# Seven-product retention projection and its gate columns: an order written out for three engines, and another way to add the attention branch in the last unit

## The chip, the core and the metric

The kernel runs on one core of one Trainium2 chip. A core has TensorE (PE, matrix products into PSUM banks), VectorE (DVE), ScalarE (ACT), GpSimd (POOL), SyncE (SP, which issues most loads) and 16 DMA engines. Each engine works through its own queue of instructions in order; engines wait for one another through semaphores. The metric is the time of one execution on the device in microseconds, lower is better. Times of several executions are given as their median with the lowest and the highest; where one execution was taken with the hardware profiler, its own time is named beside it.

## What is computed

One step of a one-layer hybrid backbone on 128 context tokens and 512 latent tokens, 640 in all, with 1024 channels, in fp32. Cut to the part that the change touches:

```python
def token_mixer(h, ...):
    q, k, v, rq, rk, rv, rg, ga, gr = split(h @ w_in)
    ya = attend_blocks(q, k_all, v_all)
    yr, s_f, s_b = retention_branch(rq, rk, rv, rg, ...)   # silu(rg) * rms_scale(o)
    y = sigmoid(ga) * (ya @ w_att_o) + sigmoid(gr) * (yr @ w_ret_o)
    return y @ w_out
```

Before it stand the conditioning, a normalisation, the attention and the retention scans; after it a gated residual, a second normalisation, a gated MLP with a width-3 convolution, another gated residual and a last normalisation. The sigmoids are computed as (1 + tanh(x/2)) with the factor one half folded into other constants. The stage of interest is `gr = h @ w_in[:, 5632:]`, `yr @ w_ret_o`, the gated sum of both branches, and the beginning of `y @ w_out`.

## The kernel before

**Numbers.** Every fp32 product is made of three reduced-precision matmuls: each operand is split into a high part (a cast) and a low part (the difference), and high x high, high x low and low x high are accumulated. So each weight block costs ScalarE a cast (L145, L1065) and VectorE a subtraction (L150, L1070) before TensorE can use it. For two of the seven products of a unit the low part is made in another way: ScalarE writes the negated value (L1067), and a DMA issued by GpSimd adds the weight to it while writing (L1068).

**Gate columns (L1031 to L1042).** The 1024 channels of `gr` are eight columns of 128. Each column is 48 matmuls of 320 tokens (two halves of 24), ScalarE takes the tanh of each half out of its bank (L1036). Weights come for two columns at a time: one load of a megabyte into a `raw` buffer (two of them, shared by all weight loads), then casts and subtractions into `wh` tiles (eight of them, shared by all weights). Between the quarters of the first columns TensorE transposes the retention output `yr` in ten blocks (`yr_blocks`), and behind column 1 `ret_sums` forms four sums of quarters of `yr` on VectorE (two or three passes each, then a cast on ScalarE and a subtraction on VectorE), with the last two rows of `thr` as scratch.

**Seven-product units (L1044 to L1157).** `yr @ w_ret_o` is a two-by-two block product done with seven products instead of eight. A unit `p` makes two columns (`f` 0 and 1) of 128 channels; there are four units, 28 products, each 12 matmuls of 320 tokens. `load` fetches a unit's weights, `prep(m)` makes the operand of one product (for four of the seven a sum of two weight quarters first, L1062), `prod(m)` runs it and takes its bank out: a copy or negated copy on ScalarE (L1096 to L1100, L1104, L1108) or an addition or subtraction on VectorE (L1102, L1105, L1111). Several products accumulate into the same bank without clearing it and are read in between, so the next product of that bank must wait until the bank has been read. `col(f)` multiplies a finished column with its gate (L1076) and then lets a GpSimd DMA add the attention branch, which was spilled to DRAM earlier as `thd`, onto it (L1077). `merge(f)` splits the finished column into the high and low operand `h2` of the next projection (L1082 on ScalarE, L1083 on VectorE).

**The order.** `seq` lists the 28 products. `ret_pump(n)` is called before the first product and after each; it emits loads and preparations as long as no more than eight prepared tiles are waiting for their product. `later` and `pend` hold a `col` for one product after the column is complete and a `merge` for eight products after. All of this is program text; what it fixes depends on the block around it. `tc.manual_schedule(engines={ET.PE})` (L1147) keeps the order of the text on TensorE alone. On the other engines, and for everything outside such a block, a planner lays the queue of each engine when the kernel is built, from its own estimate of when each instruction can start; that order is then fixed.

**Behind it.** The block ends with `gate_rows` (L1163): four groups of small matmuls into three banks, each copied out by ScalarE (L277). Then the output projection runs in two halves of 512 channels (`a_group`, L157 to L159, for the first; `out_half` for the second), its weights through the same `raw` and `wh` buffers, and the loads of the residual `x1` (L1184), of the convolution weights (L1273, L1274) and of the first block of `w_up` (L1253 casts it) queue up on SP.

Of the kernel before, what the change touches and what calls it, by code (L numbers as in the profile page):

```python
# [13 lines left out]
ALU = mybir.AluOpType  # L14
# [4 lines left out]
P = 128  # L19
# [50 lines left out]
def hybrid_step(ctx: ExitStack, tc: tile.TileContext, a: dict, o: dict):  # L70
# [937 lines left out]
    def ret_sums():  # L1008
        for m in (1, 2):
            t = f0(F32R)  # L1010
            ys[m] = [t[:, :, :HALF], t[:, :, HALF:]]
        ys[3] = [rt([P, 4, HALF], F32R) for _ in range(2)]
        x = thr[:, 6:8, :].rearrange("p a b -> p (a b)").rearrange("p (k t) -> p k t", k=4)
        q = {m: [z.bitcast(F32) for z in ya[m]] for m in ya}

        def diff(xs, zs):
            V.tensor_sub(x, xs[0], zs[0])
# [12 lines left out]

    for c in range(KD):  # L1031
        if c % 2 == 0:
            wg = load_w(w_in[:, O_GR + c * P:O_GR + (c + 2) * P], 8, 256)

        def gr_ev(hf, ts, ps, c=c):
            nc.scalar.activation(thr[:, c, ts], ps, AF.Tanh, scale=0.5)  # L1036
        for _ in b_col(wg, slice((c % 2) * P, (c % 2 + 1) * P), hTk, mm, gr_ev):
            for _ in range(2):
                next(yb, None)
        if c == 1:  # L1040
            run(yb)
            ret_sums()  # L1042

    def ret_unit(p):  # L1044
        st, ops, bs = {}, {}, {}
        u = [f1() for _ in range(2)]
        los, his = slice(0, HALF), slice(HALF, TOK)

        def load():
# [20 lines left out]
                V.tensor_sub(lo, src, hi.bitcast(F32))  # L1070
            ops[m] = (hi, lo)

        AOP = {1: ya[0, 0], 5: ys[1], 6: ys[2], 2: ya[0, 1], 7: ys[3], 4: ya[1, 1], 3: ys[4]}

        def col(f):
            V.scalar_tensor_tensor(u[f], thr[:, 2 * p + f, :], 1.0, u[f], op0=ALU.add, op1=ALU.mult)  # L1076
            nc.gpsimd.dma_start(u[f], thd[:, 2 * p + f, :], accum_op=ALU.add)  # L1077

        def merge(f):
            c = 2 * p + f  # L1080
# [4 lines left out]
        def prod(m):  # L1085
            q = {1: 1, 6: 1, 7: 1, 4: 1, 2: 2, 5: 3, 3: 3}[m]
            if m in (1, 2, 5):
                st[q] = mm([P, 512], tag="mm")[:, :HALF]
            ps, (ah, al), (bh, bl) = st[q], AOP[m], ops[m]
            for k in range(4):  # L1090
                nc.tensor.matmul(ps, bh[:, k], ah[:, k], start=m in (1, 2, 5) and k == 0, stop=False,
                                 skip_group_check=m in (3, 4, 6, 7))
                nc.tensor.matmul(ps, bh[:, k], al[:, k], start=False, stop=False, skip_group_check=m in (3, 4, 6, 7))
                nc.tensor.matmul(ps, bl[:, k], ah[:, k], start=False, stop=k == 3, skip_group_check=m in (3, 4, 6, 7))
            if m == 1:
                nc.scalar.copy(u[0][:, los], ps)  # L1096
            elif m == 5:
                nc.scalar.activation(u[1][:, his], ps, AF.Copy, scale=-1.0)
            elif m == 6:
                nc.scalar.activation(u[1][:, los], ps, AF.Copy, scale=-1.0)  # L1100
            elif m == 2:
                V.tensor_add(u[0][:, los], u[0][:, los], ps)  # L1102
            elif m == 7:
                nc.scalar.copy(u[0][:, his], ps)  # L1104
# [8 lines left out]
        return load, prep, prod  # L1113

    w_out = a["w_out"][0]
    later, pend, wo0 = [], [], []
# [13 lines left out]
    preps.append((KD // 2, 4, len(seq), lambda: wo0.append(w_split(wo0[0], 4, 512))))  # L1130
    done, loaded, live = 0, 0, []

    def ret_pump(n):
        nonlocal done, loaded
        while done < len(preps):
            g, tiles, last, fn = preps[done]
            if loaded <= min(g + 1, len(loads) - 1):
                loads[loaded]()
                loaded += 1
                continue  # L1140
            if sum(x for x, z in live if z >= n) + tiles > 8:
                return
            fn()
            live.append((tiles, last))
            done += 1

    with tc.manual_schedule(engines={ET.PE}):  # L1147
        ret_pump(0)
        for n, (p, m) in enumerate(seq):
            units[p][2](m)  # L1150
            pend.extend((n + d, fn) for d, fn in later)
            later.clear()
            ret_pump(n + 1)
            for x in [x for x in pend if x[0] <= n]:
                x[1]()
# [551 lines left out]
```

## Time and profile before

| what | value |
|---|---|
| median of 3 runs | 1203.02 us (1202.22 to 1203.61) |
| the profiled execution | 1202.9 us, of which the span from first to last instruction is 1201.1 us |
| TensorE busy | 1156.9 us, 96% of the span |
| VectorE, ScalarE, GpSimd busy | 774.7, 591.0 and 184.3 us |
| mean granted TensorE clock | 0.990 |
| gate columns | about 554.4 to 615.5 us of the span |
| seven-product units | about 615.5 to 678.9 us |
| gate rows, output projection (to the second row block of its second half) | about 678.9 to 730.8 us |

How to read the rows that follow. A row of busy time by stretch gives the stretch, its length, and the busy microseconds (with the number of instructions) of TensorE, its weight loads, VectorE, ScalarE and GpSimd, then the granted clock, the DMA engines' share and GB/s. A row of waits reads: engine, what it was about to write, line, `<-` whom it waited for, then the total, the number of times and the longest in us. A row of the timeline begins with start and duration in us; the bracket at its end is the idle time before it and what ended that. In the tables of transfers the last number is the median time from issue to landing in us. L numbers are lines of the kernel before.

### The profile page before, as it was taken

The page shows a single profiled execution, that of the slowest core. Times are in us where ns is not written, and L with a number is a line of the kernel's source. Part 1 is how long each engine was busy: PE and PEld are TensorE (multiplying, and loading weights), DVE is VectorE, ACT ScalarE, POOL GpSimd, SP SyncE. Part 2 cuts the span into 40 slices and gives each one's busy share as a digit, 9 for nine tenths or more (in the row PEclk, how much of TensorE's full clock was granted, in tenths as well). Part 3 has the DMA queues.
Part 4 walks back from the last instruction along what each step waited for, and adds up shares of the span by engine and source line. Part 5 has one row for each costly group of instructions (what it writes and reads, how often), then busy time and mean ns, then how long its engine had stood idle before and what let it go on. Part 6 is the DMA issues. An engine that isn't in the chain of part 4 may idle for free.

```text
span 1201.1 us, 18411 instructions
## 1 busy us (share of the span) xinstructions
PE 1156.9 (96%) x7269; PEld 1037.8 (86%) x7269; DVE 774.7 (64%) x1465; ACT 591.0 (49%) x1079; POOL 184.3 (15%) x193
## 2 busy tenths in 40 slices
PE   4999999999999999999998889999999999999996
PEld 4788899999988888888998767999989999899995
DVE  4566977765234436446755437977858677598887
ACT  4355655561132324444445324576657657475463
POOL 0042200000022000052022111011112112111113
PEclk9999999999999999999999998999999999999998
DMA  8742111126664431112247674536756558657553
GB/s 283 241 143 70 37 35 36 36 71 215 222 224 141 141 97 44 36 36 70 71 73 148 174 110 151 147 60 141 168 123 123 131 127 174 148 99 156 135 113 121
DMA packets 136936, 146.38 MB, mean 122 GB/s; under 512 B 26625, under 2 KB 102481, under 8 KB 136849
## 3 DMA queue, kind: packets, MB, share of 16 engines
q1 hardware_dynamic: 106592, 112.95, 29.0%
q0 software_dynamic: 30256, 32.25, 17.1%
q8 instruction: 57, 0.93, 0.3%
q14 instruction: 31, 0.25, 0.1%
HBM read 112.94 MB, written 8.65 MB: 101 GB/s over the span
## 4 chain that ended last, share of the span: by engine, by line
PE 41%; issue 5%; DVE 3%; DMA 2%; POOL 1%; ACT 1%; DVEq 0%; SPq 0%; POOLq 0%; ACTq 0%
DMA x1.u1.1_6470<-in_x_prompt 1%; DMA f1.s.14_5877<-spill.u2.2_2893 1%; POOL x1.u1.1_6470 L1194 1%; DVE acts.u2.2_97 L1222 0%; DMA f1.s.13_5876<-spill.u2.2_2893 0%; DVE acts.u1.1_96 L1221 0%; DVE x1.u1.1_6470 L1194 0%; ACT x1.u1.1_6470 L1386 0%; PE mm7.mm.45_9731 L1501 0%; PE mm7.mm.57_10483 L1501 0%; PE mm7.mm.9_7577 L1504 0%; PE mm7.mm.30_8750 L1501 0%; PE mm7.mm.42_9482 L1501 0%; PE mm7.mm.33_8999 L1501 0%; PE mm7.mm.63_10849 L1503 0%
## 5 line engine op out<-in xcount | busy, mean ns | idle before, releaser
L795 POOL DMA_DIRECT2D spill.u2.2_2893<-f1.s.1_1165 x1 | 0.6, 588 | 130.1 <-DVE mod.u4.4_2852 L586 130.1
L1515 DVE TENSOR_TENSOR t7.u4.4_7006<-t7.u4.4_7006,const.u1.1_70 128x322 f32<-128x322 f32 x10 | 4.9, 495 | 11.6 <-ACT const.u1.1_70 L1514 11.6
L888 DVE SCALAR_TENSOR_TENSOR ret2.u1.1_4329<-ret2.u1.1_4329,const.u13.13_93 64x128 f32<-64x128 f32 x24 | 6.8, 337 | 6.6 <-ACT ret2.u1.1_4329 L881 6.5
L1426 POOL TENSOR_TENSOR x1.u1.1_6470<-x1.u1.1_6470,weights.raw.422_11068 128x512 f32<-128x512 f32 x5 | 8.2, 1639 | 10.4 <-ACT x1.tm.112_11081 L1398 7.6
L890 DVE SCALAR_TENSOR_TENSOR ret2.u1.1_4329<-ret2.u1.1_4329,const.u13.13_93 64x128 f32<-64x128 f32 x24 | 6.6, 383 | 4.8 <-ACT ret2.u1.1_4329 L883 4.8
L841 DVE TENSOR_TENSOR ret.u5.5_3535<-ret.u5.5_3535,ret.u1.1_3528 128x512 f32<-128x512 f32 x5 | 3.5, 693 | 9.4 <-POOL ret.r2k.8_3713 L839 3.3
L841 DVE TENSOR_TENSOR ret.u4.4_3534<-ret.u4.4_3534,ret.u1.1_3528 128x512 f32<-128x512 f32 x5 | 3.5, 692 | 9.0 <-POOL ret.r2k.11_3893 L839 4.7
L412 ACT CAST acts.u1.1_96<-f0.s.1_109 128x640 fp32r<-128x640 f32 x4 | 2.9, 727 | 12.2 <-DVE f0.s.1_109 L410 12.2
L1068 POOL DMA_DIRECT2D weights.wh.156_5897<-weights.raw.151_5882 x1 | 1.4, 1352 | 47.3 <-ACT weights.wh.156_5897 L1067 47.3
L1254 DVE TENSOR_TENSOR gt.gt1.4_6666<-weights.raw.203_6663,gt.gt0.3_6665 128x1280 fp32r<-128x1280 f32 x1 | 1.5, 1494 | 10.9 <-ACT gt.gt0.3_6665 L1253 10.9
L565 POOL TENSOR_TENSOR p1.u1.1_609<-p1.u3.3_613,p1q.u1.1_603 128x512 f32<-128x512 f32 x1 | 1.3, 1303 | 46.4 <-DMA p1.vc.6_618<-in_cache_v 46.4
L374 PE MATMUL mm1.mm.1_167<-const.u1.1_70,xin.u1.1_108 128*128 128x128 f32 x4 | 1.1, 435 | 7.2 <-DVE xin.u1.1_108 L365 7.2
L412 ACT CAST acts.u1.1_96<-f0.s.2_110 128x640 fp32r<-128x640 f32 x4 | 2.9, 728 | 10.1 <-DVE f0.s.2_110 L410 10.1
L150 DVE TENSOR_TENSOR weights.wh.108_4359<-weights.raw.106_4356,weights.wh.107_4358 128x1024 fp32r<-128x1024 f32 x1 | 1.2, 1225 | 10.3 <-ACT weights.wh.107_4358 L145 10.3
L145 ACT CAST weights.wh.112_4514<-weights.raw.111_4512 128x1024 fp32r<-128x1024 f32 x1 | 1.1, 1050 | 13.3 <-PE mm3.mm.36_4227 L158 13.3
L950 POOL TENSOR_TENSOR f0.s.5_3532<-f0.s.5_3532,ret2.ny20.11_4911 128x512 f32<-128x512 f32 x5 | 6.0, 1236 | 9.1 <-DVE ret2.ny20.11_4911 L220 9.1
L877 POOL DMA_DIRECT2D out_new_state_ret_fwd<-ret.r2k.25_4352 x1 | 0.7, 664 | 43.8 <-ACT ret.r2k.25_4352 L876 43.8
L260 DVE COPY mod2.wr.9_4319<-aux3.aux.15_4286 128x128 f32<-128x128 f32 x1 | 0.3, 290 | 10.9 <-PE aux3.aux.15_4286 L257 10.9
L534 ACT ACTIVATE f0.s.3_715<-f0.s.3_715,p1q.ny20.11_883 128x128 f32<-128x128 f32 x20 | 6.0, 389 | 2.5 <-DVE p1q.ny20.11_883 L218 2.5
L374 PEld LDWEIGHTS mm1.mm.1_167<-const.u1.1_70,xin.u1.1_108 128*128 128x128 f32 x4 | 0.7, 218 | 7.4 <-DVE xin.u1.1_108 L365 7.4
L1392 DVE TENSOR_TENSOR x1.u1.1_6470<-x1.u1.1_6470,gate.u1.1_6441 128x512 f32<-128x512 f32 x10 | 6.7, 682 | 0.0
L145 ACT CAST weights.wh.67_3366<-weights.raw.66_3364 128x1024 fp32r<-128x1024 f32 x1 | 1.0, 1045 | 11.5 <-PE mm3.mm.8_3145 L196 11.5
(6941 smaller groups left out, 4952.0 us busy)
## 6 DMA issues: line engine op xcount, KB each, us to landing
spill.u1.1_2892<-x1.u1.1_6470 POOLq DMA_DIRECT2D x5, 512.0 KB, 3.0
xin.u1.1_108<-in_x_sample SPq DMA_DIRECT2D x4, 512.0 KB
p0.u5.5_125<-in_w_mod SPq DMA_DIRECT2D x2, 1024.0 KB
p0.u6.6_131<-in_w_mod SPq DMA_DIRECT2D x2, 1024.0 KB
p0.u7.7_134<-in_w_mod SPq DMA_DIRECT2D x2, 1024.0 KB
mod.wm.6_2920<-in_w_mod SPq DMA_DIRECT2D x1, 2048.0 KB
mod.wm.8_3073<-in_w_mod SPq DMA_DIRECT2D x1, 2048.0 KB
mod.wm.10_3230<-in_w_mod SPq DMA_DIRECT2D x1, 2048.0 KB
```

What stands on the lines that cost most here:

```text
L145: nc.scalar.copy(hi, rv)
L374: nc.tensor.transpose(xps[t, g][:, j * P:(j + 1) * P], xin[:, t, k * P:(k + 1) * P], ident)
L412: nc.scalar.copy(hT[0][:, k, :], xk)
L534: nc.scalar.activation(x[:, j], x[:, j], AF.Copy, scale=rstd[:, j:j + 1])
L841: V.tensor_mul(z, z, r1[:, t, 0:1, :].to_broadcast([P, 8, 64]))
L888: V.scalar_tensor_tensor(Ss[0:64, hh, st + 1, j], Ss[0:64, hh, st, j], cdsel[0:64, h:h + 1], Ss[0:64, hh, st + 1, j], op0=ALU.mult, op1=AL ...
L890: V.scalar_tensor_tensor(Ss[64:128, hh, 2 - st, j], Ss[64:128, hh, 3 - st, j], cdsel[64:128, h:h + 1], Ss[64:128, hh, 2 - st, j], op0=ALU. ...
L950: nc.gpsimd.tensor_mul(ov, ov, rso[:, 4 * t:4 * t + 4].unsqueeze(2).to_broadcast([P, 4, P]))
L1194: (V if g else nc.gpsimd).tensor_add(x1[:, t, gs], x1[:, t, gs], tm)
L1392: V.tensor_mul(x1[:, t, gs], x1[:, t, gs], gb[:, t == 0, gs])
L1426: eng.tensor_mul(x, x, fg[:, c0:c0 + 512])
L1515: V.tensor_sub(u[1][:, hi_u], u[1][:, hi_u], u3[i])
```

## The change

Three things change in the text, all between the retention scans and the output projection.

1. The block with a fixed order now names three engines, TensorE, VectorE and ScalarE, and begins before the gate columns instead of behind them. The columns' loop is rewritten inside it: weights are loaded one pair of columns ahead (`wgr`) and split behind the even column before; all ten transposed blocks go into column 0, three to a quarter; `ret_sums` becomes a generator that makes one sum behind each of the columns 1 to 4.
2. `ret_pump` gets an argument `room`. It is called behind column 5 to load the first unit's weights and behind column 6 to prepare its first four operands, then before the first product as before.
3. The last unit no longer lets a DMA add the attention branch: behind product 15 `reload` loads the two columns of `thd` plainly through SP into two tiles `tl`, and `col` adds them on VectorE.

```diff
@@ ret_sums: one sum, then a yield @@
             V.tensor_sub(ys[m][1], x, ys[m][0].bitcast(F32))
+            yield
@@ the columns, before @@
-    for c in range(KD):
-        if c % 2 == 0:
-            wg = load_w(w_in[:, O_GR + c * P:O_GR + (c + 2) * P], 8, 256)
-        for _ in b_col(wg, slice((c % 2) * P, (c % 2 + 1) * P), hTk, mm, gr_ev):
-            for _ in range(2):
-                next(yb, None)
-        if c == 1:
-            run(yb)
-            ret_sums()
+    def wgr(c):
+        return w_raw(w_in[:, O_GR + c * P:O_GR + (c + 2) * P], 8, 256)
@@ ret_unit @@
+        tl = []
         def col(f):
             V.scalar_tensor_tensor(u[f], thr[:, 2 * p + f, :], 1.0, u[f], op0=ALU.add, op1=ALU.mult)
-            nc.gpsimd.dma_start(u[f], thd[:, 2 * p + f, :], accum_op=ALU.add)
+            if tl:
+                V.tensor_add(u[f], u[f], tl[f])
+            else:
+                nc.gpsimd.dma_start(u[f], thd[:, 2 * p + f, :], accum_op=ALU.add)
+
+        def reload():
+            for f in range(2):
+                tl.append(f1())
+                nc.sync.dma_start(tl[f], thd[:, 2 * p + f, :])
@@ ret_pump @@
-    def ret_pump(n):
+    def ret_pump(n, room=8):
...
-            if loaded <= min(g + 1, len(loads) - 1):
+            if loaded <= min(g + (n >= 0), len(loads) - 1):
...
-            if sum(x for x, z in live if z >= n) + tiles > 8:
+            if sum(x for x, z in live if z >= n) + tiles > room:
@@ the block @@
-    with tc.manual_schedule(engines={ET.PE}):
+    wg = load_w(w_in[:, O_GR:O_GR + 2 * P], 8, 256)
+    sums = ret_sums()
+    with tc.manual_schedule(engines={ET.PE, ET.DVE, ET.Activation}):
+        for c in range(KD):
+            if c % 2 == 0 and c + 2 < KD:
+                graw = wgr(c + 2)
+            for _ in gr_col(c, wg):
+                if c == 0:
+                    for _ in range(3):
+                        next(yb, None)
+            if c:
+                next(sums, None)
+            if c % 2 == 0 and c + 2 < KD:
+                wn = w_split(graw, 8, 256)
+            elif c + 1 < KD:
+                wg = wn
+            if c == KD - 3:
+                ret_pump(-1, 0)
+            if c == KD - 2:
+                ret_pump(-1, 4)
         ret_pump(0)
         for n, (p, m) in enumerate(seq):
             units[p][2](m)
             pend.extend((n + d, fn) for d, fn in later)
             later.clear()
+            if n == 15:
+                units[-1][3]()
             ret_pump(n + 1)
```

`gr_col` is the same column with the same tanh as before; the dictionary of the seven right-hand operands is now built inside `prod`, since the sums do not exist yet when a unit is set up. The number of matmuls, casts, sums and evacuations is the same; two accumulating DMAs become two plain loads and two additions on VectorE.

More of the change, by code (lines that the diff above doesn't have):

```diff
@@ L1029, in ret_sums, with gr_col, ev @@
             V.tensor_sub(ys[m][1], x, ys[m][0].bitcast(F32))
[L1031 to L1042 removed]
+            yield
+    def wgr(c):
+        return w_raw(w_in[:, O_GR + c * P:O_GR + (c + 2) * P], 8, 256)
+    def gr_col(c, w):
+        def ev(hf, ts, ps):
+            nc.scalar.activation(thr[:, c, ts], ps, AF.Tanh, scale=0.5)
+        yield from b_col(w, slice((c % 2) * P, (c % 2 + 1) * P), hTk, mm, ev)
     def ret_unit(p):
@@ L1111, in prod @@
                 V.tensor_sub(u[1][:, los], u[1][:, los], ps)
-        return load, prep, prod
+        return load, prep, prod, reload
     w_out = a["w_out"][0]
```

4 lines of the change are left out of this document (2 added, 2 removed).

## The prediction

> **What bounds the kernel now.** First the page's busy table and granted clock, then three windows cut at the borders of the changed stage (gate columns, seven-product units, first output projection).
>
> ```profile
> PE 1156.9 (96%) x7269; PEld 1037.8 (86%) x7269; DVE 774.7 (64%) x1465; ACT 591.0 (49%) x1079; POOL 184.3 (15%) x193
> ...
> PEclk9999999999999999999999998999999999999998
> ```
> ```profile
> 615.50:678.90 63.40, 53.85 (x342) 52.85 (x341) 37.49 (x62) 31.25 (x64) 14.12 (x13) 0.95 0.71 143
> 678.90:730.80 51.90, 46.90 (x200) 37.07 (x199) 17.73 (x32) 14.31 (x27) 9.82 (x12) 0.90 0.71 151
> 554.40:615.50 61.10, 60.89 (x425) 60.61 (x424) 39.14 (x38) 26.50 (x43) 3.05 (x4) 1.00 0.19 57
> ```
>
> TensorE sets the time almost everywhere. The gate columns (554.4 to 615.5) leave it 0.2 us idle: nothing is to be won there. The units (615.5 to 678.9) leave 9.55 us, the stage behind them 5.0 us, both at a clock below 1. TensorE's waits, longest first:
>
> ```profile
> PE mm3.mm.72_6288 L1091 <- ACT f1.s.16_5879 L1100: 4.1, 1, 4.1
> PE mm3.mm.69_6154 L1091 <- ACT f1.s.14_5877 L1100: 3.9, 1, 3.9
> PE mm3.mm.80_6677 L157 <- ACT weights.wh.199_6655 L145: 2.9, 1, 2.9
> PE mm3.mm.72_6288 L1091 <- ACT f1.s.15_5878 L1104: 1.6, 1, 1.6
> PE mm3.mm.80_6677 L158 <- DVE weights.wh.200_6656 L150: 1.3, 1, 1.3
> PE mm3.mm.80_6677 L158 <- DVE x1.tm.16_6669 L1229: 0.5, 1, 0.5
> ...
> PE mm3.mm.80_6677 L157 <- ACT weights.wh.201_6659 L145: 0.3, 1, 0.3
> ```
>
> Each row says which matmul waited, for whom, and for how long. Three waits in the units (4.1, 3.9, 1.6) are for a bank that ScalarE had not emptied; the four of mm.80, 5.0 us together, belong to the stage behind. The timeline shows why ScalarE was late the first time, and the transfers' table how long such a transfer takes from issue to landing:
>
> ```profile
> 643.76 0.89 POOL L1077 DMA_DIRECT2D f1.s.12_5875<-spill.u2.2_2893  x1 [4.60 <-DVE f1.s.12_5875 L1076]
> ...
> 650.70 0.82 ACT L1082 CAST acts.u1.1_96<-f1.s.12_5875 128x128 fp32r<-128x128 f32 x2 [4.65 <-DMA f1.s.12_5875<-spill.u2.2_2893]
> ...
> 652.48 0.43 ACT L1100 ACTIVATE f1.s.14_5877<-mm3.mm.69_6154 128x320 f32<-128x320 f32 x1
> ```
> ```profile
> f1.s.14_5877<-spill.u2.2_2893 POOLq DMA_DIRECT2D x1, 320.0 KB, 7.0
> f1.s.13_5876<-spill.u2.2_2893 POOLq DMA_DIRECT2D x1, 320.0 KB, 4.5
> ...
> f1.s.15_5878<-spill.u2.2_2893 POOLq DMA_DIRECT2D x1, 320.0 KB, 8.1
> ```
>
> A merge cast (L1082) stands at the head of ScalarE's queue and waits until 650.70 for the transfer that GpSimd issued at 643.76, an accumulation onto the column (they land after 4.5 to 8.1 us). ScalarE works its queue in order, so the evacuation at 652.48, whose bank TensorE had filled before its wait of 3.9 us began, is late though nothing but its place in the queue held it. VectorE and ScalarE are busy 37.5 and 31.3 of the 63.4 us: order, not load, costs here. The product rate, read off TensorE's timeline:
>
> ```profile
> 674.43 0.54 PE L157 MATMUL mm3.mm.75_6483<-weights.wh.184_6348,acts.u1.1_96 128*128 128x512 f32 x1
> ...
> 677.27 0.31 PE L1093 MATMUL mm3.mm.72_6288<-yr.u2.2_5319,weights.wh.183_6285 128*128 128x320 f32 x1
> 677.42 0.31 PE L1094 MATMUL mm3.mm.72_6288<-yr.u1.1_5318,weights.wh.183_6285 128*128 128x320 f32 x1
> ...
> 678.88 1.05 PE L275 MATMUL aux3.aux.87_6442<-const.u1.1_70,const.u5.5_85 128*128 128x128 f32 x8
> ...
> 682.37 0.48 PE L157 MATMUL mm3.mm.75_6483<-weights.wh.184_6348,acts.u1.1_96 128*128 128x512 f32 x1
> ```
>
> Matmuls follow one another in 0.147 us (677.27, 677.42), so 28 products of 12 need 49.4 us. Of 63.4 us, 9.6 are waits, 0.7 are three projection matmuls run early (from 674.43), and 3.7 are left for the lowered clock.
>
> **The change, part by part.** *Gate columns.* TensorE has the same instructions, in a fixed order. On VectorE that order puts a column pair's weight split (two subtractions behind ScalarE's casts) after an operand sum (two or three passes, a cast, a subtraction).
>
> ```profile
> 573.85 1.22 DVE L150 TENSOR_TENSOR weights.wh.143_5647<-weights.raw.141_5644,weights.wh.142_5646 128x1024 fp32r<-128x1024 f32 x1
> 574.99 1.48 DVE L1017 TENSOR_TENSOR rt.u1.1_5323<-yr.u1.1_5318 128x1280 f32<-128x1280 f32 x1
> ```
>
> Carried along the columns (48 matmuls, 7.04 us each, the ten transposed blocks inside column 0) with 1.48 a pass and 1.22 a subtraction, the splits are ready near 586.1 and 600.3, for columns that start at 586.9 and 601.0. TensorE's work hides them: cost 0; once that cover of 0.7 us is gone, it pays every further microsecond. The first weights of the units are prepared behind column 6, where TensorE is busy with the last one.
>
> *Units.* ScalarE and VectorE now follow the text: merges stand eight products (14 us) behind their product, past the 8.1 us of the slowest accumulation, so the 9.6 us of waits go, and the 3.7 of low clock with them. What is late next: the preparations, in which VectorE and ScalarE wait for one another.
>
> ```profile
> 620.73 0.62 ACT L1065 CAST weights.wh.163_5951<-weights.raw.152_5884 128x512 fp32r<-128x512 f32 x1 [1.06 <-DVE weights.raw.152_5884 L1062]
> ...
> 622.10 0.63 ACT L1067 ACTIVATE weights.wh.164_5967<-weights.raw.152_5884 128x512 fp32r<-128x512 f32 x1
> ```
> ```profile
> 619.95 0.69 DVE L1062 TENSOR_TENSOR weights.raw.152_5884<-weights.raw.152_5884 128x512 f32<-128x512 f32 x1
> 621.38 0.69 DVE L1070 TENSOR_TENSOR weights.wh.163_5951<-weights.raw.152_5884,weights.wh.163_5951 128x512 fp32r<-128x512 f32 x1 [0.74 <-ACT weights.wh.163_5951 L1065]
> ...
> 627.25 0.82 DVE L1076 SCALAR_TENSOR_TENSOR f1.s.10_5873<-rt.u1.1_5323,f1.s.10_5873 128x640 f32<-128x640 f32 x1
> ```
>
> Sum, cast and subtraction take 2.1 us from 619.95 to 622.07, handing over between engines in 0.03 to 0.09; a product takes 1.76. I carried all 28 products with these durations and 0.06 a hand-over, from 615.5. Three waits come out. The pump ahead of the first product puts three casts, one negated cast and VectorE's sum before the first evacuation: the third product wants its bank at 619.0 and gets it at 620.7, 1.7 us. Product 17 waits 0.5, the last 0.7. In the third unit VectorE's list takes 14.7 us against TensorE's 12.3; the lead of eight prepared tiles absorbs it and no unit is left to build on it. The products end at 615.5 + 49.4 + 2.9 = 667.8, against 678.88: **11.1 us earlier**.
>
> *Last unit.* Two plain 320 KB loads join SP's queue once unit 0's merges free their tiles (near 652); they are wanted near 670. No row shows a plain load of that size: the accumulation of the same bytes took 4.5 at least, raw.203's megabyte below 9.4 us (705.31 to 714.71, behind conv_w); I take 6, nothing to 9.4 being the bounds, and 18 are free. Cost 0; if that cover goes, the last merges wait. Behind them in SP's queue only w_out's next block, wanted at 666, is near. Two VectorE additions (about 0.8 each, as L1076) replace two accumulations, so the last merges wait for VectorE instead of 4.5 to 8.1 us of transfer; TensorE wants their result only half a projection (60 matmuls of 0.232, 14 us) later, which hid it before too.
>
> *Gate rows.* Their four copies now stand behind four merges on ScalarE, the second of which waits for the accumulation issued near 666 (landing 670.5 to 674). With three banks, TensorE would wait 4.2 to 6.1 us for the fourth block. Row 674.43 shows that projection matmuls are put into such holes; I take 1.5 us, nearer to that row than to an unfilled hole; bounds 0 and 6.1 (plus about 1.5 of low clock).
>
> *Behind it.* The next wait hangs on another chain:
>
> ```profile
> 679.76 1.22 DVE L150 TENSOR_TENSOR weights.wh.192_6555<-weights.raw.188_6548,weights.wh.191_6554 128x1024 fp32r<-128x1024 f32 x1
> ...
> 681.01 0.37 SPq L134 DMA_DIRECT2D weights.raw.198_6653<-in_w_out  x1
> ...
> 685.62 16.01 SPq L1273 DMA_DIRECT2D t7.u5.5_7011<-in_conv_w  x3
> ...
> 705.31 3.56 SPq L134 DMA_DIRECT2D weights.raw.203_6663<-in_w_up  x1
> ...
> 714.71 1.26 ACT L1253 CAST gt.gt0.3_6665<-weights.raw.203_6663 128x1280 fp32r<-128x1280 f32 x1 [10.38 <-DMA weights.raw.203_6663<-in_w_up]
> ...
> 717.23 1.03 ACT L145 CAST weights.wh.199_6655<-weights.raw.198_6653 128x1024 fp32r<-128x1024 f32 x1
> ...
> 718.32 0.51 PE L157 MATMUL mm3.mm.80_6677<-weights.wh.199_6655,acts.u1.1_96 128*128 128x512 f32 x1 [2.87 <-ACT weights.wh.199_6655 L145]
> ...
> 721.17 0.63 PE L157 MATMUL mm3.mm.80_6677<-weights.wh.199_6655,acts.u1.1_96 128*128 128x512 f32 x1
> 721.60 0.63 PE L158 MATMUL mm3.mm.80_6677<-weights.wh.200_6656,acts.u1.1_96 128*128 128x512 f32 x1
> ...
> 730.38 0.40 PE L159 MATMUL mm3.mm.81_6690<-weights.wh.201_6659,acts.u2.2_97 128*128 128x512 f32 x1
> ```
>
> The last product frees the tile of wh.192, whose subtraction lets SP issue at 681.01, 2.1 us after the products; conv_w holds SP for 16 us; raw.203 follows, its cast waits for it at ScalarE's head until 714.71, and the cast of wh.199, for which TensorE waits, is behind that one. With products ending at 667.8 this chain is 11.1 us earlier: TensorE resumes at 707.2 instead of 718.32. TensorE itself would be ready at 667.8 + 36.6 (from 678.88 to the start of the 2.87 us wait) + 0.7 + 1.5 = 706.6. The chain still sets it, by 0.6 us, and I leave what follows up to 730.8 as it is, low clock included, since the chain's start and the gate wait are known to a few microseconds only. The profile keeps TensorE busy nearly to the end, so the gain stays: 1202.9 (the profiled execution: span 1201.1 and 1.8 around it; the median shown, 1203.02, is 0.1 more) - 11.1 = 1191.8 us.
>
> **Rivals.** *Full clock behind the short wait*: before, TensorE stood 2.87 us, then 1.33, and ran at 0.43 us a matmul (721.17, 721.60) where 0.23 is full; after the 1.6 us wait it ran at 0.147. If the remaining wait is as short, the tail takes 1.3 + 0.5 + 0.3 of waits and 24 x 0.232 = 7.7 instead of 12.5 us: 1187.0. The Trainium skill ("TensorE: Matmul & The Clock Gate", Part 1) says the gate knows half and full clock alone and judges free-running windows of about 3.4 us; by that rule a wait near 1 us keeps full clock and this rival holds, while the 2.87 + 1.33 us here fit it only taken together.
>
> *TensorE alone sets it*: if the cast of raw.203 no longer stands ahead of wh.199, 36.6 + 24 x 0.232 = 42.2 us of work follow the products, with 0.7 and 1.5: 712.2 against 730.8, so 1184.3. For it: that stall needs one cast ahead of another; against it: ScalarE's order there comes from the same planner.
>
> *The chain starts late*: wh.192's subtraction falls behind the last merges on VectorE (near 676.5): SP issues at 677.7, 3.3 us earlier than before: 1199.6. For it: VectorE's list is full there; against it: before, the same subtraction was put between two columns' work.
>
> *Slower*: the lockstep. Each preparation hands over twice; carried at 0.3 a hand-over the products end near 676, at 0.4 near 681, at 0.5 near 687. It decides from about 0.35; at 0.5 the kernel takes 1210.9. The rows' 0.03 to 0.09 speak against it, that the order of all later work is laid anew speaks for some of it.
>
> *No change*: the merges come due too early still, waits move but stay: 1203.
>
> **How the numbers follow.** Forecast 0.34, full clock 0.20, TensorE alone 0.11, late chain 0.15, no change 0.06, slower 0.14. Range 1183 to 1202: all but the slower case and the ends of two others. Faster by over 0.2% (2.4 us, about what a measurement here can tell from none) 0.80, within it 0.06, slower 0.14.
>
> **What would show it.** Right: no wait of TensorE over 2 us between first and last product, no merge cast waiting on a transfer in the first three units, products ending near 668 at clock 1.00, one wait of 1 to 2 us at the third product, SP's conv_w issue near 674.5. Wrong: waits at every product (lockstep), a wait over 3 us at the fourth gate block, columns 4 or 6 waiting for a split, or the wait at wh.199 grown.

## The result and the profile after

The changed kernel takes 1183.77 us (median of 4 runs, 1183.52 to 1184.35), the kernel before 1202.76 (4 runs, 1202.22 to 1203.61): ratio 0.9842, 95% interval 0.9825 to 0.9859, 19.0 us. A second comparison of the same two kernels, with other experiments, gave 0.988 (0.9862 to 0.9898); what is known of the difference stands at the end. The forecast was 1191.8, in a range of 1183 to 1202. The profiled execution took 1183.9 us, its span 1182.1. L numbers below are lines of the changed kernel (product L1095, merge cast L1085, operand sum L1059, cast L1062) and, in the rows of an experiment, of that experiment's kernel.

The busy time by stretch, cut at the same three borders as before (gate columns, units, behind them):

```profile
553.30:614.00 60.70, 60.70 (x426) 60.67 (x425) 38.72 (x37) 25.57 (x41) 1.78 (x3) 1.00 0.16 53
614.00:666.90 52.90, 50.59 (x340) 49.72 (x340) 36.33 (x59) 31.08 (x63) 15.53 (x15) 1.00 0.86 182
666.90:711.80 44.90, 42.80 (x200) 34.48 (x199) 20.12 (x34) 15.77 (x31) 8.06 (x9) 1.00 0.76 162
```

| stretch | before, us | after, us | difference |
|---|---|---|---|
| start of the span to the columns | 554.4 | 553.3 | -1.1 |
| gate columns | 61.1 | 60.7 | -0.4 |
| units | 63.4 | 52.9 | -10.5 |
| gate rows and first projection | 51.9 | 44.9 | -7.0 |
| the rest of the span | 470.3 | 470.3 | 0.0 |

The first line is no work of the change: every engine's list is the same up to there, and the start of the columns lay between 552.8 and 554.4 us in all profiles. The gain sits in two places: the units, where it was forecast, and the stage behind them, where none was. TensorE's waits in these stages, longest first:

```profile
PE mm3.mm.63_5918 L1095 <- ACT f1.s.9_5324 L1100: 1.4, 1, 1.4
PE mm3.mm.80_6681 L157 <- ACT weights.wh.201_6663 L145: 1.3, 1, 1.3
PE mm3.mm.72_6292 L1095 <- ACT f1.s.15_5330 L1108: 0.9, 1, 0.9
PE mm3.mm.80_6681 L158 <- DVE x1.tm.16_6673 L1254: 0.8, 1, 0.8
```

Of the three long waits of the units two short ones are left (third and last product), and the wait for wh.199 is gone. The timeline, with the rows that answer to those of before:

```profile
641.98 0.82 ACT L1085 CAST acts.u1.1_96<-f1.s.10_5325 128x128 fp32r<-128x128 f32 x2
...
663.62 1.05 ACT L145 CAST weights.wh.189_6554<-weights.raw.188_6552 128x1024 fp32r<-128x1024 f32 x1 [2.35 <-DMA weights.raw.188_6552<-in_w_out]
664.57 0.42 ACT L1108 COPY f1.s.15_5330<-mm3.mm.72_6292 128x320 f32<-128x320 f32 x1
...
668.42 0.37 SPq L134 DMA_DIRECT2D weights.raw.198_6657<-in_w_out  x1
...
671.55 14.18 SPq L1298 DMA_DIRECT2D t7.u5.5_7015<-in_conv_w  x3
...
689.42 3.71 SPq L134 DMA_DIRECT2D weights.raw.203_6667<-in_w_up  x1
...
698.16 1.26 ACT L1278 CAST gt.gt0.3_6669<-weights.raw.203_6667 128x1280 fp32r<-128x1280 f32 x1 [5.49 <-DMA weights.raw.203_6667<-in_w_up]
...
700.69 1.04 ACT L145 CAST weights.wh.199_6659<-weights.raw.198_6657 128x1024 fp32r<-128x1024 f32 x1
...
703.63 0.40 PE L157 MATMUL mm3.mm.80_6681<-weights.wh.199_6659,acts.u1.1_96 128*128 128x512 f32 x1
```

The merge cast at 641.98 has no bracket: its transfer had landed, and nothing behind it is held up. In the kernel before, all eight merge casts waited for their transfer, for 1.87 to 7.12 us; here a single one does, the last of the third unit, for 1.04 us at 669.29, behind the products. Further down stands the chain that was to set the end: raw.203 is issued at 689.42 instead of 705.31, its cast runs at 698.16 instead of 714.71, and wh.199 is ready before TensorE comes to it at 703.63.

### The profile page after: what moved, and what is told of

Same layout as the page of the kernel before. It is cut to its first block, busy times and chain, and to the rows that moved or that the text cites. A ratio compares the mean times of both kernels' runs of the same rounds, so it can differ in the third digit from the quotient of the medians.

```text
span 1182.1 us, 18414 instructions
## 1 busy us (share of the span) xinstructions
PE 1148.7 (97%) x7269; PEld 1031.4 (87%) x7269; DVE 775.6 (66%) x1467; ACT 590.9 (50%) x1079; POOL 182.9 (15%) x191
## 4 chain that ended last, share of the span: by engine, by line
PE 87%; DVE 5%; issue 3%; ACT 2%; DMA 1%; POOL 1%; SPq 0%; DVEq 0%; POOLq 0%; ACTq 0%
DMA x1.u1.1_6474<-in_x_prompt 1%; POOL x1.u1.1_6474 L1219 1%; DMA weights.raw.188_6552<-in_w_out 0%; POOL f0.s.5_3532 L950 0%; DVE acts.u2.2_97 L1247 0%; DMA xin.u1.1_108<-in_x_sample 0%; DVE x1.u1.1_6474 L1219 0%; DVE acts.u1.1_96 L1246 0%; DVE acts.u2.2_97 L415 0%; PE mm1.mm.11_300 L159 0%; PE mm7.mm.45_9735 L1526 0%; PE mm7.mm.9_7581 L1529 0%; PE mm7.mm.57_10487 L1526 0%; PE mm7.mm.54_10218 L1526 0%; PE mm7.mm.33_9003 L1526 0%
## 5 line engine op out<-in xcount | busy, mean ns | idle before, releaser
L150 DVE TENSOR_TENSOR weights.wh.108_4359<-weights.raw.106_4356,weights.wh.107_4358 128x1024 fp32r<-128x1024 f32 x1 | 1.2, 1225 | 10.3 <-ACT weights.wh.107_4358 L145 10.3
L412 ACT CAST acts.u1.1_96<-f0.s.2_110 128x640 fp32r<-128x640 f32 x4 | 2.9, 729 | 10.1 <-DVE f0.s.2_110 L410 10.1
```

The lines of the kernel that those rows point to most:

```text
L150: (lo_eng or V).tensor_sub(lo, rv, hi.bitcast(F32))
L412: nc.scalar.copy(hT[0][:, k, :], xk)
```

## The experiments

The stages of each profile, cut by the same borders (first product, end of the last product, end of the second row block of the second half). Idle is the length of the stretch less TensorE's busy time, so a busy time well above 50 us in the units, or 43 us behind them, means a lowered clock.

| kernel | ratio to before, interval | units: idle, busy | behind: idle, busy |
|---|---|---|---|
| before | 1 | 9.6, 53.9 | 5.0, 46.9 |
| changed | 0.9842 (0.9825 to 0.9859) | 2.3, 50.6 | 2.1, 42.8 |
| e1, VectorE to the planner | 0.9848 (0.9836 to 0.9861) | 0.0, 50.4 | 2.0, 44.3 |
| e2, ScalarE to the planner | 0.9916 (0.9903 to 0.9928) | 5.3, 52.3 | 2.4, 42.8 |
| e3, no reload | 0.9912 (0.9899 to 0.9925) | 1.4, 50.4 | 7.5, 44.5 |
| e4, old gate columns | 0.9853 (0.984 to 0.9866) | 0.6, 50.3 | 1.8, 42.8 |
| e5, before with conv_w early | 0.9933 (0.992 to 0.9946) | 9.8, 55.0 | 0.0, 42.0 |
| e6, changed with conv_w early | 0.9816 (0.9803 to 0.9829) | 1.4, 50.5 | 0.1, 42.2 |
| e7, changed with conv_b three times | 0.9953 (0.9939 to 0.9966) | 2.9, 50.6 | 13.0, 46.6 |
| e8, six tiles ahead | 0.9866 (0.9852 to 0.9879) | 1.9, 50.9 | 1.8, 44.3 |
| f1, changed again | 0.988 (0.9862 to 0.9898) | 2.3, 50.6 | 2.5, 42.8 |
| f2, before with the reload | 0.9964 (0.9949 to 0.998) | 8.9, 53.6 | 3.1, 44.6 |
| f3, ScalarE's order and the reload | 0.9846 (0.9831 to 0.9862) | 0.0, 50.0 | 2.2, 42.9 |
| f4, e1 with conv_w early | 0.9806 (0.9791 to 0.982) | 0.6, 50.4 | 0.0, 42.2 |

### Whose order pays: e1, e2, e4

e1 and e2 each give one engine back to the planner, e4 puts the loop of the gate columns back as it was and fixes the units alone.

```diff
-    with tc.manual_schedule(engines={ET.PE, ET.DVE, ET.Activation}):
+    with tc.manual_schedule(engines={ET.PE, ET.Activation}):      # e1
+    with tc.manual_schedule(engines={ET.PE, ET.DVE}):             # e2
```
```diff
+    for c in range(KD):                              # e4, ahead of the block
+        if c % 2 == 0:
+            wg = load_w(w_in[:, O_GR + c * P:O_GR + (c + 2) * P], 8, 256)
...
+        if c == 1:
+            run(yb)
+            run(ret_sums())
     with tc.manual_schedule(engines={ET.PE, ET.DVE, ET.Activation}):
-        for c in range(KD):
...
```

> The changed kernel with the order of VectorE in the gate columns and the units left to the planner again; TensorE and ScalarE stay as written, and ScalarE's list of instructions is the same as in the changed kernel. Theory (ScalarE's place for the merge casts is what pays in the units): within 1.5 us of the changed kernel's 1183.8. Rival (VectorE's order is what pays): 8 to 12 us of the 19 come back, 1192 to 1196, with waits of 3 us and more for products.

> The changed kernel with the order of ScalarE left to the planner; TensorE and VectorE stay as written. ScalarE's list then has the merge casts of unit 0 some five to ten of its instructions earlier. Theory (merge casts too early): the second merge of unit 0 stands behind an evacuation near 639, its accumulation is issued near 637.2 and lands 4.5 to 8.1 us later, so ScalarE waits 2.6 to 6.2 us at its head and two evacuations behind it are late; the same at the second merge of unit 1. TensorE loses 2 to 8 us: 1186 to 1192. Rival (VectorE's order is what pays, or the lead of prepared tiles absorbs it): within 1 us of 1183.8.

> The changed kernel with the gate columns as they were before (weights split and operand sums where the planner puts them, no early preparation of the first weights); only the units' block is fixed on three engines. Theory (the fixed columns are worth nothing, TensorE is busy there in both): within 1.5 us of 1183.8, the difference at the first products, whose weights are prepared later. Rival (the early preparation behind the columns is what keeps ScalarE and VectorE ahead): 3 to 6 us more, 1187 to 1190, as waits at the first four products.

All three ran on one chip: e1 1181.8 us, e4 1182.7, e2 1189.8 (before 1200.2). So neither VectorE's order nor the new columns carry the gain; ScalarE's order does, for 8 us of it. e2's timeline shows by what means:

```profile
635.04 1.46 POOL L1075 DMA_DIRECT2D f1.s.9_5324<-spill.u2.2_2893  x1
...
641.27 0.82 ACT L1085 CAST acts.u1.1_96<-f1.s.9_5324 128x128 fp32r<-128x128 f32 x2 [3.87 <-DMA f1.s.9_5324<-spill.u2.2_2893]
...
642.52 0.42 ACT L1100 COPY f1.s.13_5328<-mm3.mm.69_6154 128x320 f32<-128x320 f32 x1
...
642.99 0.42 PE L1095 MATMUL mm3.mm.69_6154<-f0.s.8_5529,weights.wh.171_6077 128*128 128x320 f32 x1 [0.76 <-ACT f1.s.13_5328 L1100]
...
652.22 1.72 POOL L1075 DMA_DIRECT2D f1.s.11_5326<-spill.u2.2_2893  x1
...
658.81 0.82 ACT L1085 CAST acts.u1.1_96<-f1.s.11_5326 128x128 fp32r<-128x128 f32 x2 [4.69 <-DMA f1.s.11_5326<-spill.u2.2_2893]
...
661.00 0.42 ACT L1102 ACTIVATE f1.s.16_5331<-mm3.mm.73_6312 128x320 f32<-128x320 f32 x1
...
661.48 0.41 PE L1095 MATMUL mm3.mm.73_6312<-yr.u1.1_5318,weights.wh.181_6253 128*128 128x320 f32 x1 [2.40 <-ACT f1.s.16_5331 L1102]
```

The second merge of a unit stands at ScalarE's head until its accumulation has landed, 6.2 and 6.6 us after GpSimd issued it; the evacuation behind it (642.52, 661.00) is late, and TensorE waits 0.76 and 2.40 us for that bank. A third wait, 2.2 us for the last product, has the same shape: the first merge of the third unit waits 4.50 us at ScalarE's head until 667.52, and the evacuation stands behind it. It is the picture of before, with shorter waits.

e1 has no wait of TensorE among the products at all, though ScalarE's list is the same as in the changed kernel. The wait at the third product therefore came from VectorE's written order. First the timeline of the changed kernel there:

```profile
616.20 0.69 DVE L1067 TENSOR_TENSOR weights.wh.158_5906<-weights.raw.151_5778,weights.wh.158_5906 128x512 fp32r<-128x512 f32 x1 [2.57 <-ACT weights.wh.158_5906 L1062]
616.81 0.69 DVE L1059 TENSOR_TENSOR weights.raw.151_5778<-weights.raw.151_5778 128x512 f32<-128x512 f32 x1
...
617.59 0.62 ACT L1062 CAST weights.wh.159_5910<-weights.raw.151_5778 128x512 fp32r<-128x512 f32 x1 [1.42 <-DVE weights.raw.151_5778 L1059]
...
618.63 0.42 ACT L1100 COPY f1.s.9_5324<-mm3.mm.63_5918 128x320 f32<-128x320 f32 x1
```

The same instructions in the timeline of e1, without wh.158's subtraction:

```profile
613.97 0.69 DVE L1059 TENSOR_TENSOR weights.raw.151_5778<-weights.raw.151_5778 128x512 f32<-128x512 f32 x1
...
616.98 0.62 ACT L1062 CAST weights.wh.159_5910<-weights.raw.151_5778 128x512 fp32r<-128x512 f32 x1
...
618.03 0.41 ACT L1100 COPY f1.s.9_5324<-mm3.mm.63_5918 128x320 f32<-128x320 f32 x1
```

As written, the sum for wh.159 stands behind the subtraction of wh.158, which waits for ScalarE's cast; ScalarE then waits 1.42 us for that sum ahead of the evacuation (618.63). In e1 the planner put the same sum at 613.97, and the evacuation runs 3.1 us after the first product began instead of 4.6.

### The reload: e3, f2

e3 is the changed kernel without the reload, f2 the kernel before with the reload and nothing else.

```diff
-            if n == 15:                 # e3 takes it out, f2 puts it in
-                units[-1][3]()
```

> The changed kernel without the plain loads in the last unit: it accumulates by GpSimd's transfer as the other units do. Theory of the prediction (the reload hides nothing that was not hidden: TensorE wants the result half a projection later): within 1 us of 1183.8. Rival (the last two merge casts stand ahead of the gate copies on ScalarE and would wait for transfers issued near 670 and 671, landing 674.5 to 679, while TensorE's fourth gate block wants its bank at 673.8): TensorE waits 2 to 6 us there, 1186 to 1190.

> The kernel before with the plain loads and the two additions in the last unit, and nothing else; TensorE's list is the same, ScalarE's too but for two pairs of neighbours. Theory (the reload pays only where the order as written puts the gate copies behind the last merges; before, the planner had them ahead): within 1.5 us of 1201.5. Rival (the transfers at the end of the last unit were on the path before too, and the 7.1 us that the changed kernel loses without the reload are to be had here as well): 1194 to 1197.

e3 takes 1189.7 us, 7.9 more than e1, which ran on the same chip (the changed kernel itself did not; by the ratios to the kernel before, 0.9912 and 0.9842, e3 takes 8.4 us more). The prediction's "cost 0" for this step is refuted, as the timeline of e3 at the end of the last unit shows:

```profile
669.42 0.86 POOL L1075 DMA_DIRECT2D f1.s.16_5331<-spill.u2.2_2893  x1 [4.25 <-DVE f1.s.16_5331 L1071]
670.37 0.86 POOL L1075 DMA_DIRECT2D f1.s.15_5330<-spill.u2.2_2893  x1
...
670.72 17.41 SPq L1296 DMA_DIRECT2D t7.u5.5_7011<-in_conv_w  x3
...
677.75 0.82 ACT L1085 CAST acts.u1.1_96<-f1.s.16_5331 128x128 fp32r<-128x128 f32 x2 [8.22 <-DMA f1.s.16_5331<-spill.u2.2_2893]
...
680.68 0.82 ACT L1085 CAST acts.u1.1_96<-f1.s.15_5330 128x128 fp32r<-128x128 f32 x2 [2.11 <-DMA f1.s.15_5330<-spill.u2.2_2893]
681.40 0.58 ACT L277 COPY gate.u1.1_6441<-aux3.aux.87_6442 128x512 f32<-128x512 f32 x1
...
682.03 2.08 PE L275 MATMUL aux3.aux.90_6460<-const.u1.1_70,const.u5.5_85 128*128 128x128 f32 x8 [7.50 <-ACT gate.u1.1_6441 L277]
...
695.26 0.37 SPq L134 DMA_DIRECT2D weights.raw.203_6663<-in_w_up  x1
```

The last two accumulations land 8.3 and 10.3 us after their issue, the two merge casts wait for them at ScalarE's head, and the gate copies, which the written order puts behind these, come at 681.40; TensorE waits 7.50 us for a bank, although 24 projection matmuls had filled the first part of that hole. f2 was expected to show nothing, since the planner had two gate copies ahead of the last merges. It shows 4.0 us (1197.4 against 1201.4): the theory missed, the rival was nearly right. In the profile 4.2 us come from the stage behind the products (47.7 instead of 51.9) and 0.9 from the units. What gets faster behind the products is the chain of loads, the way from their end to the issue of raw.203 (the timeline of f2, SP's rows for conv_w and raw.203):

```profile
682.58 14.23 SPq L1284 DMA_DIRECT2D t7.u5.5_7015<-in_conv_w  x3
...
700.38 3.61 SPq L134 DMA_DIRECT2D weights.raw.203_6667<-in_w_up  x1
```

From the end of the products (676.5) that is 23.9 us; before it was 26.4, in the changed kernel 22.5. (In e3 it is 29.2, but there SP was free at 691.8 and waited 3.4 us more for the buffer of raw.203, which came free late because TensorE was 7.50 us late.) Three loads of conv_w hold SP for 16.0 us before and 17.41 in e3, where the last accumulations run beside them, and for 14.23 in f2 and 14.18 in the changed kernel, where they don't.

### The chain behind: e5, e6, e7

e5 and e6 move the loads of conv_w and conv_b to 511 us, where SP is free (a small copy on VectorE keeps them from starting earlier); e7 loads conv_b three times instead of once.

```diff
+    cw = cp([P, 4, 2 * NF])                          # e5, e6: behind the retention scans
+    V.tensor_copy(cw[:, :, 0], rvv[0][:, 0, 0, 0:4])
+    for i in range(3):
+        nc.sync.dma_start(cw[:, i, :], a["conv_w"][0, i].rearrange("(c p) -> p c", p=P))
+    nc.sync.dma_start(cw[:, 3, :], a["conv_b"][0].rearrange("(c p) -> p c", p=P))
...
+    for _ in range(2):                               # e7: behind the load of conv_b
+        nc.sync.dma_start(cw[:, 3, :], a["conv_b"][0].rearrange("(c p) -> p c", p=P))
```

> The kernel before with one thing moved: the four loads of conv_w and conv_b go out some 180 us earlier, where SP has nothing to do, into a tile of their own. All other engines keep their lists. Theory (these loads hold SP's queue for 19.7 us ahead of raw.203, whose cast stands ahead of wh.199): raw.203 is issued near 686, its cast runs near 695, wh.199 is ready near 698, before TensorE wants it at 715; the waits of 2.9, 1.3 and part of 0.5 go and the clock stays full, 4.8 more: 1193 to 1195. Rival (the clock is low there because of the waits in the units): only the waits go, 1197.5 to 1199. Rival (that stall hangs on something else than SP's queue): within 1 us of 1202.8.

> The same move in the changed kernel. Theory (the earlier end of the products already took raw.203 out of TensorE's way; the last waits of 1.3 and 0.8 stand behind squares on ScalarE, not behind SP): within 1 us of 1183.8. Rival (SP's queue still sets the end of the stage): 1.5 to 2.5 us faster.

> The changed kernel with the load of conv_b given three times instead of once, ahead of raw.203: SP's queue is held about 7.1 us longer (3.54 each); all other lists stay. In the changed kernel the cast of wh.199 ends at 701.7 and TensorE wants it at 703.6, so 1.9 us are free. Theory (SP's chain comes back as the bound): TensorE waits about 5.2 us at wh.199, loses the 2.0 us of waits behind it no longer, and runs the rest of the stage at a low clock: 1187 with full clock, 1192 with 4.8 us of low clock. Rival (TensorE alone sets the stage and the chain has more room than the trace shows): within 1 us of 1183.8.

e5 fits the theory: 0.9933, 8.0 us by the ratio (6.9 by the medians), TensorE busy without a gap and at full clock behind the units, while the units kept long waits (4.1, 3.0, 1.9 and 0.8 us) and cost 1.5 us more. So the low clock behind the units does not come from the waits in them. A detail was wrong. raw.203 goes out at 698.01, not near 686, as its timeline shows:

```profile
696.76 1.23 DVE L150 TENSOR_TENSOR weights.wh.197_6656<-weights.raw.193_6649,weights.wh.196_6655 128x1024 fp32r<-128x1024 f32 x1 [0.18 <-ACT weights.wh.196_6655 L145]
...
698.01 0.38 SPq L134 DMA_DIRECT2D weights.raw.203_6669<-in_w_up  x1
...
704.21 1.25 ACT L1258 CAST gt.gt0.3_6671<-weights.raw.203_6669 128x1280 fp32r<-128x1280 f32 x1
```

With SP free, the load waits for its buffer: it goes out when the last subtraction that reads raw.193 ends (696.76 + 1.23). conv_w and conv_b cost 7.3 us here (705.31 less 698.01), not the 19.7 of its rows.

e6 was expected to gain nothing and gained: 0.9816, 3.1 us by the ratios, and in the profile 2.6 us behind the units, 1.0 in them, 1.4 in the rest of the span. The two waits that I had put down to squares on ScalarE (the sums of squares for the second normalisation) went as well. In the changed kernel they hang on raw.203 too, by way of VectorE: VectorE's subtraction for raw.203 waits for that cast (699.46), the product of the next row block stands behind it (701.74), GpSimd adds that product, the square waits 3.02 us for the addition (704.75), and the cast of wh.201 stands behind the square (705.38). In e6, with the cast of raw.203 at 691.06 instead of 698.16, the cast of wh.201 runs at 699.19. This chain is read from the order of the queues; no run tries it by itself.

e7 brings the chain back, more than intended. Its longest wait of TensorE, and SP's rows of its timeline:

```profile
PE mm3.mm.80_6681 L157 <- ACT weights.wh.199_6659 L145: 11.1, 1, 11.1
```

```profile
689.80 3.61 SPq L1299 DMA_DIRECT2D t7.u5.5_7015<-in_conv_b  x1
698.17 6.14 SPq L1301 DMA_DIRECT2D t7.u5.5_7015<-in_conv_b  x2
704.40 3.29 SPq L134 DMA_DIRECT2D weights.raw.203_6667<-in_w_up  x1
```

The two additional loads did not follow the first at 693.4. All three loads of conv_b write the same place, and the profile has SP wait, before each of the two, until the load before it had landed, 10.0 us in all; the row at 698.17 shows the two together. With that, raw.203 is issued 15.0 us later than in the changed kernel and the cast of wh.199 ends 14.5 later; less the 1.9 that were free and the 1.5 by which TensorE itself came later, that is the 11.1 us of the row. The chain's slack in the changed kernel was 1.9 us, as the trace had it.

### The third product: e8

```diff
-        ret_pump(0)
+        ret_pump(0, 6)
```

> The changed kernel with two preparations fewer ahead of the first product: the evacuation of the first product stands ahead of them on ScalarE. Theory (the wait of 1.4 us at the third product is the evacuation's place behind two preparations): it goes and nothing takes its place, 1182.2 to 1182.8. Rival (ScalarE and VectorE are late by those two preparations in any order): the wait moves to a later product, within 0.5 us of 1183.8.

The wait at the third product went and the units stayed at 52.8 us, as the rival had it, though not for its reason. e8 takes 1185.7 us, ratio 0.9866, slower than either forecast: behind the units it ran in part at the lower clock (busy 44.3). The last product now waits for longer (1.59 us instead of 0.88), and three rows of its timeline name the reason:

```profile
664.03 1.04 ACT L145 CAST weights.wh.189_6554<-weights.raw.188_6552 128x1024 fp32r<-128x1024 f32 x1 [3.06 <-DMA weights.raw.188_6552<-in_w_out]
664.98 0.42 ACT L1108 COPY f1.s.15_5330<-mm3.mm.72_6292 128x320 f32<-128x320 f32 x1
...
665.45 0.42 PE L1095 MATMUL mm3.mm.72_6292<-yr.u1.1_5318,weights.wh.183_6289 128*128 128x320 f32 x1 [1.59 <-ACT f1.s.15_5330 L1108]
```

A weight cast at ScalarE's head waits 3.06 us for the load of raw.188, and the evacuation of that bank stands behind it. That load did not come earlier with the products: SP waited 10.1 and 1.4 us for GpSimd's transfers that make wh.180 and wh.181 from the buffer it was to fill (10.2 and 1.4 in the changed kernel). So being early only meant waiting there.

### Together: f1, f3, f4

f3 is the kernel before with ScalarE's order in the units and the reload, nothing else of the change; f4 joins e1 and e6.

```diff
-    with tc.manual_schedule(engines={ET.PE}):
+    with tc.manual_schedule(engines={ET.PE, ET.Activation}):
...
+            if n == 15:
+                units[-1][3]()
```

> The changed kernel as it is, once more, so that the three beside it are compared on one chip. Expected: ratio to the kernel before 0.983 to 0.986 and the same stages as in its first profile (columns 60.7 us, units 52.9, behind 44.9), unless the clock falls behind the waits of 1.3 and 0.8 us, which would add about 2 us.

> The kernel before with two parts of the change alone: the units' order fixed on TensorE and ScalarE, and the reload. Gate columns, operand sums and first preparations stand where the planner puts them, VectorE is left to the planner everywhere. Theory (these two parts are the whole gain): ratio 0.982 to 0.986, units of 50 to 52 us with no wait of over 1 us, behind them 44 to 47. Rival (the fixed columns, the early preparation or VectorE's order carry a part): 3 to 8 us more, ratio 0.987 to 0.992.

> The changed kernel with VectorE left to the planner and the loads of conv_w and conv_b moved to where SP has nothing to do. Theory (VectorE's written order costs the 1.4 us at the third product, SP's queue the two waits behind the units and what follows them): units 50.4 us, behind them 42 to 43 with no wait of over 0.5 us, the rest 469: 1176 to 1178 on a chip where the kernel before takes 1202, ratio 0.978 to 0.981. Rival (the two gains are one, since both end in the same wait): as with the loads moved alone, ratio 0.9816.

On one chip: before 1201.4, the changed kernel 1186.2, f3 1182.3, f4 1177.8. These two parts of the change are the whole gain, as the theory said; with VectorE left to the planner the products run without a wait in e1 and f3, and with one of 0.6 us, the last, in f4. f1 has the stages of the first profile but not its ratio (0.988, expected 0.983 to 0.986). f4 came out as forecast and beats both kernels: 23.6 us less than before by the medians, ratio 0.9806, with 0.6 us of idle TensorE from the first product to the end of the stage.

## Why the prediction was right or wrong

**Gate columns at cost 0: right.** 61.1 us became 60.7; e4, which has the old ones, is as fast. The splits were ready at 585.8 and 599.8, forecast 586.1 and 600.3, and no column waited.

**Units, 11.1 us earlier: right to 0.6 us.** The waits behind merge casts went with ScalarE's order (e1, e2), and the 3.7 us of low clock with them. Of the three new waits, the third product took 1.4 (forecast 1.7), product 17 none (0.5), the last 0.9 (0.7). The first has the reason that the step gave only in part: it takes VectorE's written place of a sum and the casts ahead of the evacuation together, since it goes when the sum moves (e1, with the same casts) and when two preparations fewer stand ahead (e8). The last is no lag of the preparations: rows 663.62 and 664.57 show a weight cast waiting 2.35 us for raw.188 ahead of the evacuation. That its size came out near is luck.

**The reload at cost 0, "which hid it before too": wrong.** Priced at nothing, it is worth 4.0 us by itself (f2) and some 8 with the order as written (e3). Before, the last accumulations were not hidden: without them the chain to raw.203 is 2.5 us shorter (f2). With the order as written they would cost 7.5 us at the fourth gate block (e3). The step looked only at who reads their result, not at what stands behind the waiting cast on ScalarE, nor at the loads that share the time of the transfers.

**Gate rows, 1.5 us: off by that much.** 17 projection matmuls filled the hole and nothing was lost. Its reading, copies behind merges that may wait for a transfer, was right and is what e3 shows; it was priced for the wrong merge, since the reload takes away the two that wait longest.

**Behind it: the step that failed.** "With products ending at 667.8 this chain is 11.1 us earlier", and "I leave what follows up to 730.8 as it is, low clock included". The cast of raw.203 came 16.55 us earlier, and the sum of the rows says why: 12.0 from the end of the products (678.88 to 666.91), 0.6 from there to the issue of raw.198 (2.1 to 1.5), 1.5 from there to conv_w (4.6 to 3.1), 1.8 from conv_w itself (16.01 to 14.18) and 0.7 from raw.203 to its cast (9.4 to 8.7). The 1.5 and the 1.8 belong to the reload: f2, which has it alone, shows the same two (3.1 and 14.23). TensorE needed wh.199 only 11.8 us earlier than its old start at 715.45, at 703.63, so the wait of 2.87 went, with it 1.33 at wh.200, and the matmuls behind ran at 0.23 us instead of 0.43: busy 42.8 us instead of 46.9. That is 7.0 us that the forecast left out, and nearly the whole of its error of 8.

**The rivals.** *Full clock* named what happened to the clock, but kept a short wait at wh.199 and the 1.3 us at wh.200, and neither was there. *TensorE alone* has the right time, 1184.3, for another reason than it gave: the cast of raw.203 still stands ahead of wh.199 and is only early enough. The measured time lies 0.8 us inside the lower end of the range, which of all cases only this rival came near; that the range holds is in part luck. *Late chain*: the subtraction of wh.192 ran at 667.16, among the merges, not behind them. *Lockstep* and *no change*: no product but two waited. Of the signs named, two came out differently: a merge cast of the third unit did wait for its transfer (1.04 us), and conv_w went out at 671.55, not near 674.5.

## What to carry to other kernels

When a shortened stage feeds a chain of loads, walk that chain link by link at its new time: each link can shrink too, and a stall that shrinks below TensorE's own work vanishes with the low clock behind it. In an in-order queue, ask of each instruction that waits for a transfer what stands behind it; here a merge cast cost nothing by itself and up to 7.5 us through the copies behind it. Fix the order of the one engine whose queue goes wrong, and try the others unfixed: two parts of this change did as much as all of it.

## What the runs showed of the hardware

**The clock after short waits is a toss.** e1 and the changed kernel have the same two waits ahead of the end of the first projection, 1.2 to 1.3 and 0.8 us, yet run on at different rates. TensorE's timeline in e1, behind both waits:

```profile
707.23 0.63 PE L159 MATMUL mm3.mm.80_6681<-weights.wh.201_6663,acts.u2.2_97 128*128 128x512 f32 x1
707.65 0.63 PE L157 MATMUL mm3.mm.81_6694<-weights.wh.199_6659,acts.u1.1_96 128*128 128x512 f32 x1
708.08 0.63 PE L158 MATMUL mm3.mm.81_6694<-weights.wh.200_6660,acts.u1.1_96 128*128 128x512 f32 x1
```

And in the changed kernel, behind its two:

```profile
708.52 0.39 PE L158 MATMUL mm3.mm.80_6681<-weights.wh.202_6664,acts.u1.1_96 128*128 128x512 f32 x1
708.75 0.39 PE L159 MATMUL mm3.mm.80_6681<-weights.wh.201_6663,acts.u2.2_97 128*128 128x512 f32 x1
708.98 0.40 PE L157 MATMUL mm3.mm.81_6694<-weights.wh.199_6659,acts.u1.1_96 128*128 128x512 f32 x1
```

0.43 us a matmul in e1 for about 3.3 us, 0.23 in the changed kernel. e4 and e8 part in the same way: both wait 0.9 and 0.8 us there, and TensorE's busy time behind the units is 42.8 us in e4 and 44.3 in e8. Five runs of e1 fall in two groups, 1181.4 to 1181.8 us at a mean clock of 0.997 to 0.998 and 1183.8 and 1183.9 at 0.994 and 0.995; f1's five go the same way, 1184.7 and 1184.8 at 0.997 and 1186.2 to 1188.3 at 0.995 and 0.996, which lifts its median by about 1.5 us. Where the slow stretch lies is seen in the profiled execution alone; for the others it is taken from their mean clock. The two ratios of the changed kernel differ by 4.6 us, and the other 3 or so stay open. The Trainium skill ("TensorE: Matmul & The Clock Gate", Part 1) says that the gate judges windows of about 3.4 us that run free of the kernel. The length of the slow stretch and the toss agree with it; its statement that half clock follows at least one idle window does not, since e1 idled 2.0 us in all; nor does what the prediction took from it, that a wait near 1 us keeps full clock, where two follow one another within 1.3 us.

**Loads in small pieces hold SP's queue longer beside other transfers.** The same three loads of conv_w, 22 KB each in some 5,600 packets, held SP for 7.3 to 7.6 us in the quiet place (e5, e6, f4), 13.5 to 15.6 in the kernels with the reload, and 16.0 and 17.4 beside the accumulations. In e5 the DMA engines moved 7 GB/s meanwhile, in the kernel before 218.

**An accumulation's time varies, and no run here shows with what.** 320 KB landed in 4.5 to 8.1 us before, and in 8.3 and 10.3 us at the end of e3's last unit, where conv_w ran beside them. But the last one of e5, with no load of conv_w near, took 8.5, and the same one before, with them, 8.1.
